# A float32 transformer trunk on one Trainium2 core: five opening blocks in each feed-forward layer instead of four, head stacks made in one step, and four other moves of work between queues

## The chip, the cores and the metric

The kernel runs on one core of a Trainium2 chip. The core has a matrix engine (PE, whose weight loads are shown as PEld), a vector engine (DVE), a scalar engine (ACT), a general engine (POOL), a queue that issues transfers (SP) and 16 DMA engines. The metric is the device time in microseconds (us) of one execution; the time before is the median of three runs. All products are in float32, made of three matmuls on rounded parts (below).

## The reference

Two layers over 512 tokens of width 1024. Each layer is a feed-forward part (SwiGLU), a token mixer, and a second feed-forward part, each between two RMS norms and with a residual:

```python
def swiglu(h, w_in, w_out):
    gu = h @ w_in
    g, u = jnp.split(gu, 2, axis=-1)
    return (jax.nn.silu(g) * u) @ w_out
...
for layer in range(DEPTH):
    g = norm_gain[layer]
    h = swiglu(rms_norm(x, g[0]), ffn_w_in[layer, 0], ffn_w_out[layer, 0])
    x = x + 0.5 * rms_norm(h, g[1])
    h = token_mixer(rms_norm(x, g[2]), mix_w_in[layer], conv_w[layer], conv_b[layer],
                    gate_bias[layer], mlstm_norm_gain[layer], mix_w_out[layer])
    x = x + rms_norm(h, g[3])
    h = swiglu(rms_norm(x, g[4]), ffn_w_in[layer, 1], ffn_w_out[layer, 1])
    x = x + 0.5 * rms_norm(h, g[5])
```

The hidden width of the feed-forward part is 2816, that is 22 tiles of 128, called f = 0 to 21 here. The mixer projects 1024 to 3600 columns, runs eight heads of windowed attention and four heads of a recurrent memory (mLSTM), and projects back.

## The kernel before

**Split numbers.** Every factor is split into a high part (ACT casts it, `hi` or `xh`) and a low part (DVE subtracts the high part from the original, `lo` or `xl`). A product is three matmuls: high by high, high by low, low by high. Weights arrive in `raw` buffers of 512 KB (three of them, and three each of `hi` and `lo`, used in turn), so a fresh load waits until an older tile is split, and a fresh split until PE is through with an older tile. The helper for the mixer's weights is `split_w` (cast L114, subtraction L115), that for the opening blocks `halves_of` (L97, L99).

**Tokens and the chain.** The 512 tokens are four tiles t = 0 to 3. At the end of each part `chain` does for each t: the norm behind the part (`post`: squares on ACT L163, gain on DVE L166, update of `xs` L170), the norm ahead of the next part (`pre`: squares on ACT L181, a power on POOL L136, scaling into `nt` on DVE L185, eight transposes `tr` on PE L191), and `put`, which copies the transposed tile out of its PSUM bank as `xh` (ACT L209), `xl` (DVE L210) and, ahead of a feed-forward part, as the exact copy `xf` (ACT L236, t 0 and 1) and as sums and differences of t and t-2 (`tq`, L228, L229). The power on POOL and two small steps before it (`rs_u`, `rs_v`) and after it (`rs_a`, `rs_y`) make the inverse root.

**The first matmul of a feed-forward part (`ffn_in`).** The first `ne` tiles f are the openings. `block(f, left)` multiplies both weight tiles of f (gate, then up) with the tokens of t 0 and 1, later `block(f, right)` with those of t 2 and 3: 48 matmuls of 256 columns each, so 96 for a tile f. The left blocks need only t 0 and 1 and can run while the chain of t 2 and 3 is made. The other tiles go through `seven`, which takes seven products of 12 matmuls, 84 in all, instead of eight, by working with sums of weights (`ws`, made on DVE in L320 to L323) and sums of tokens (`tq`, `xf`). A tile of `seven` is prepared during the one ahead of it; the first one (`now = Weights(ne)`) is prepared ahead of the loop. Its up-weight goes to a buffer `wu` in slot 17 or 19, by the parity of f:

```python
raw = chunk("wu", 17 + 2 * (f % 2)) if gu and not whole_f else raw_tile()
```

The same two slots hold `xf`: slot 17 the copy for the first half of the width, which `finish` (L228, L229, called behind the right blocks) reads last, and slot 19 the copy for the second half, whose last reader is t 3's `put` (L245).

**The mixer.** It begins with four groups of columns (`proj_nat`, PSUM name `nat`) for t 0 and 1, while t 2 and 3 of the chain are made; then `mixer_proj_T` (`projT`), which needs all tokens, then the groups for t 2 and 3 and the gates (`mixer_gates`), in which PE transposes small rows (`gnat`, L727). The attention needs for each of four head pairs a stack of keys and one of queries (`stack`, `stk`, `kst`, `qsh`, `qsl`): four transposes each, and copies out of the bank on ACT and DVE, of 64 partitions. `stack_pair` yields between keys and queries; the loop over 32 score tiles (`sc`) takes these steps at n = 2, 4, 9, 11, 16 and 18.

**Order.** A scheduler that simulates the engines lays out each engine's instructions, except in the loop over `seven`, which keeps the written order. `tc.issue_after(i)` holds what is issued in it behind instruction i.

Of the kernel before, what the change touches and what calls it, by code (L numbers as in the profile page):

```python
# [41 lines left out]
def trunk_kernel(ctx, tc, x, norm_gain, ffn_w_in, ffn_w_out, mix_w_in, conv_w, conv_b,  # L42
# [59 lines left out]
    def split_w(load, n, k4, pieces=1):  # L102
        raw = raw_tile()
        hi = wp.tile([P, 1056], F32R, tag="hi", name="hi", bufs=3)
        lo = wp.tile([P, 1056], F32R, tag="lo", name="lo", bufs=3)
        m = n * k4

        def view(w):
            return w[:, :m].rearrange("p (k c) -> p k c", k=k4)
        step = k4 // pieces  # L110
        for k in range(0, k4, step):
            r, h, l = [view(w)[:, k: k + step] for w in (raw, hi, lo)]
            load(r, k)
            A.copy(h, r)  # L114
            V.tensor_tensor(l, r, h.bitcast(F32), ALU.subtract)  # L115
        return view(hi), view(lo)
# [144 lines left out]
    def ffn_in(layer, j, xx, late=None):  # L261
# [20 lines left out]
        def block(f, c, pieces=1, after=None):  # L282
            h = h_of(f) if hts[f] is None else hts[f]
            banks = []
            for gu in range(2):
                lo_k, hi_k = halves_of(load(f, gu, pieces, True)[:, :1024], 1024, after)
                ps = psA("gu")[:, c]
                for q, w2 in enumerate((lo_k, hi_k)):
                    product(ps, w2, [x[:, 4 * q: 4 * q + 4, c] for x in (xx.h, xx.l)], q == 0)
                banks.append(ps)  # L290
# [93 lines left out]
        ne = 4  # L384
        for f in range(ne):
            block(f, left, 2 if late and f == 0 else 1, first_nt[-1] if late and f == 0 else None)
# [98 lines left out]
    def proj_nat(layer, xx, col, n, evac, tiles=range(NT), ps_of=None, per=1):  # L485
# [3 lines left out]
        for q in range(2):  # L489
            def load(dst, _, q=q):  # L490
                nc.sync.dma_start(dst, w[:, q * 4: q * 4 + 4, col: col + n])
            parts.append(split_w(load, n, 4))
# [37 lines left out]
    def mixer(layer, xx):  # L530
# [42 lines left out]
        for n, g in enumerate(groups):  # L573
            run(proj_nat(layer, xx, *g, tiles=(0, 1), per=1 + (n in (1, 2))))
# [4 lines left out]
        for n, g in enumerate(groups[1:]):  # L579
            run(proj_nat(layer, xx, *g, tiles=(2, 3), per=1 + (n < 2)))  # L580
            if n == 1:
# [39 lines left out]
        def stack_pair(hp):  # L621
# [3 lines left out]
            yield  # L625
# [4 lines left out]
            yield  # L630
# [22 lines left out]
        def opening():  # L653
            for n, _ in enumerate(heads()):
                if n == 58:
                    run(stack_pair(0))
# [179 lines left out]
    def stack(src, hp, dh, dl):  # L836
# [9 lines left out]
        else:  # L846
            for e, s, o in ((0, lo, hi), (1, hi, lo)):
# [3 lines left out]
                A.copy(dl[o, e], dl[s, e].bitcast(F32))  # L851

    def attention(stack_pair, stacks, pts, av, mask, mm):
# [54 lines left out]
        for n in range(32 + lead + 1):  # L908
            if n < 32:
                scores(n)  # L910
                if n in (2, 9, 16):
                    made = stack_pair(1 + n // 7)
                if n in (2, 4, 9, 11, 16, 18):
                    next(made)
# [24 lines left out]

    def start(t, xx=xx):  # L940
        load_x(t, 1)
        chain(t, None, xx, False)
# [4 lines left out]
    for t in range(2):  # L947
        chain(t, None, xx, False)
    late = [lambda: start(2), lambda: start(3)]
# [61 lines left out]
```

## Time and profile before

| what | value |
|---|---|
| median of three runs | 2122.14 us (2122.1 to 2124.03) |
| profiled execution | 2122.1 us, span of its instructions 2120.1 us, so 2.0 us lie around the span |
| PE busy | 2041.7 us (96%) |
| DVE busy | 1544.4 us (73%) |
| ACT busy | 1154.5 us (54%) |
| POOL busy | 253.6 us (12%) |
| DMA | 270.28 MB, mean 127 GB/s |

The page puts PE at 96%, so whatever shortens the kernel is found in the other 78 us, or in stretches in which PE is busy but slow. For that two views are read: who PE waited for, and stretches of equal length with the number of matmuls that PE did in each. The count is the better measure, since a matmul at a lowered clock is counted as busy time too. Line numbers are those of the kernel before.

### The profile page before, as it was taken

Reading aid. Unit: us, or ns where it says so; the run is one execution under the profiler, and the core shown is the slowest. Engines: PE = TensorE matmul, PEld = TensorE weight load, DVE = VectorE, ACT = ScalarE, POOL = GpSimd, SP = SyncE. Lnnn points to the kernel's source line nnn. Section 1 sums busy time; section 2 is a strip of 40 time slices with the busy share of each in tenths; the row PEclk is TensorE's granted clock in tenths of the full one; section 3 lists DMA queues with packets and bytes.
Section 4 is the critical chain, followed back from the end, with each engine's and each line's share of the span. In section 5 each row is a group of like instructions: output and inputs, shape, how many; then the busy total and the mean of one; then the engine's idle time right before and its main releaser. Section 6 shows DMA issues by size and latency. Waiting matters only on the chain. (4 is left out here: it accounts for less than half of the span.)

```text
span 2120.1 us, 35561 instructions
## 1 busy us (share of the span) xinstructions
PE 2041.7 (96%) x13870; PEld 1861.2 (88%) x13870; DVE 1544.4 (73%) x2634; ACT 1154.5 (54%) x2058; POOL 253.6 (12%) x330
## 2 busy tenths in 40 slices
PE   8899999999999989999998999999999999899998
PEld 7899988889977889998898999888899779899886
DVE  7688757685767878876687886667856677788665
ACT  5455555445665645555554555554456755455554
POOL 1000001233512100000010000003434220000000
PEclk9999999999999999999999999999999999999999
DMA  7433355541113633335663334564411235333364
GB/s 217 123 111 100 110 188 193 143 122 58 53 51 119 190 110 107 113 102 187 188 188 107 105 100 129 188 192 126 119 53 41 88 122 160 110 104 115 120 205 144
DMA packets 297566, 270.28 MB, mean 127 GB/s; under 512 B 8661, under 2 KB 267189, under 8 KB 297398
## 3 DMA queue, kind: packets, MB, share of 16 engines
q1 hardware_dynamic: 297398, 268.01, 41.8%
q8 instruction: 108, 1.77, 0.3%
q14 instruction: 60, 0.49, 0.1%
HBM read 265.88 MB, written 2.10 MB: 126 GB/s over the span
## 5 line engine op out<-in xcount | busy, mean ns | idle before, releaser
L115 DVE TENSOR_TENSOR lo<-raw,hi 128x1024 fp32r<-128x1024 f32 (+1 forms) x280 | 348.8, 1246 | 241.4 <-ACT hi L114 241.3
L114 ACT CAST hi<-raw 128x1024 fp32r<-128x1024 f32 (+1 forms) x280 | 294.5, 1053 | 311.0 <-PE o L419 225.6
L417 PE MATMUL o<-lo,hq 128*128 128x512 f32 x704 | 236.9, 394 | 0.8 <-DVE lo L115 0.8
L419 PE MATMUL o<-hi,hq 128*128 128x512 f32 x704 | 223.3, 394 | 0.0
L416 PE MATMUL o<-hi,hq 128*128 128x512 f32 x704 | 210.6, 395 | 2.5 <-ACT hq L453 2.5
L297 ACT CAST hi<-ws 128x1024 fp32r<-128x1024 f32 x144 | 151.2, 1052 | 70.9 <-ACT a L297 62.1
L255 PE MATMUL pa<-tq,hi 128*128 128x256 f32 x576 | 164.6, 286 | 22.3 <-ACT hi L297 22.3
L500 PE MATMUL nat<-hi,xh 128*128 128x256 f32 (+1 forms) x640 | 184.9, 291 | 0.0
L501 PE MATMUL nat<-lo,xh 128*128 128x256 f32 (+1 forms) x640 | 182.0, 285 | 2.9 <-DVE lo L115 2.9
L502 PE MATMUL nat<-hi,xl 128*128 128x256 f32 (+1 forms) x640 | 181.6, 285 | 0.0
L299 DVE TENSOR_TENSOR lo<-ws,hi 128x1024 fp32r<-128x1024 f32 x144 | 175.2, 1219 | 1.5 <-ACT hi L297 1.5
L257 PE MATMUL pa<-tq,lo 128*128 128x256 f32 x576 | 165.0, 286 | 1.9 <-DVE lo L299 1.9
L256 PE MATMUL pa<-tq,hi 128*128 128x256 f32 x576 | 164.8, 286 | 0.0
L255 PE MATMUL pc<-xh,hi 128*128 128x256 f32 x576 | 163.6, 284 | 0.0
L257 PE MATMUL pc<-xh,lo 128*128 128x256 f32 x576 | 163.4, 284 | 0.0
L256 PE MATMUL pc<-xl,hi 128*128 128x256 f32 x576 | 163.4, 284 | 0.0
L416 PEld LDWEIGHTS o<-hi,hq 128*128 128x128 f32 x704 | 131.9, 188 | 34.0 <-ACT hq L453 3.4
L417 PEld LDWEIGHTS o<-lo,hq 128*128 128x128 f32 x704 | 131.9, 188 | 31.5 <-DVE lo L115 1.1
L419 PEld LDWEIGHTS o<-hi,hq 128*128 128x128 f32 x704 | 132.3, 188 | 30.8
L256 PE MATMUL gu<-xl,hi 128*128 128x256 f32 x512 | 147.4, 289 | 6.6 <-DVE xl L210 6.6
L255 PE MATMUL gu<-xh,hi 128*128 128x256 f32 x512 | 146.8, 290 | 4.6 <-ACT xf L236 3.7
L257 PE MATMUL gu<-xh,lo 128*128 128x256 f32 x512 | 146.3, 288 | 0.0
(242 smaller groups left out, 5660.3 us busy)
## 6 DMA issues: line engine op xcount, KB each, us to landing
raw<-in_ffn_w_out_dram SPq DMA_DIRECT2D x176, 512.0 KB, 3.5
raw<-in_ffn_w_in_dram SPq DMA_DIRECT2D x138, 512.0 KB, 3.9
wu<-in_ffn_w_in_dram SPq DMA_DIRECT2D x68, 512.0 KB, 4.0
raw<-in_mix_w_in_dram SPq DMA_DIRECT2D x56, 512.0 KB, 3.8
raw<-in_mix_w_out_dram SPq DMA_DIRECT2D x32, 512.0 KB, 3.7
raw<-in_mix_w_in_dram SPq DMA_DIRECT2D x16, 528.0 KB, 3.7
gpost<-in_norm_gain_dram SPq DMA_DIRECT2D x6, 512.0 KB, 5.9
gpre<-in_norm_gain_dram SPq DMA_DIRECT2D x5, 512.0 KB, 4.7
```

The source lines that it names most:

```text
L114: A.copy(h, r)
L115: V.tensor_tensor(l, r, h.bitcast(F32), ALU.subtract)
L255: PE.matmul(ps, wh[:, k], xh[:, k], start=start and k == 0, stop=False, skip_group_check=True)
L256: PE.matmul(ps, wh[:, k], xl[:, k], start=False, stop=False, skip_group_check=True)
L257: PE.matmul(ps, wl[:, k], xh[:, k], start=False, stop=k == 3, skip_group_check=True)
L299: V.tensor_tensor(lo, src, fp(hi), ALU.subtract)
L416: PE.matmul(banks[t][n], a, wh[:, n], start=first, stop=False)
L417: PE.matmul(banks[t][n], a, wl[:, n], start=False, stop=False)
L419: PE.matmul(banks[t][n], b, wh[:, n], start=False, stop=end)
L500: PE.matmul(d, xh[:, k, tok], wh[:, k % 4], start=k == 0, stop=False)
L501: PE.matmul(d, xh[:, k, tok], wl[:, k % 4], start=False, stop=False)
L502: PE.matmul(d, xl[:, k, tok], wh[:, k % 4], start=False, stop=k == NK - 1)
```

## The change

- `ne` is 5 instead of 4: one more tile f in each of the four feed-forward parts goes through left and right blocks, one fewer through `seven`, and the first `Weights` is that of f = 5, whose `wu` lies in slot 19.
- At the start of the program, the chains of t 2 and 3 are held behind the last ACT instruction of t 1's chain (the second half's `xf` copy), and the low part of the first up-weight behind t 1's last DVE instruction.
- In the mixer's first four groups the low part of each second half of a weight is made on POOL instead of DVE.
- The second half of `mixer_gates` is called behind the last of the right-hand groups instead of the last but one.
- `stack_pair` makes keys and queries in one step, at n = 3, 13 and 17; in the query stacks the second copy of the low part is a subtraction on DVE (L850's form) instead of a copy on ACT (L851).

```diff
@@ -99,7 +99,7 @@
             V.tensor_tensor(lo[:, :n], src, hi[:, :n].bitcast(F32), ALU.subtract)
         return [[w[:, q: q + 512].rearrange("p (k c) -> p k c", k=4) for w in (hi, lo)] for q in range(0, n, 512)]
 
-    def split_w(load, n, k4, pieces=1):
+    def split_w(load, n, k4, sub=None, pieces=1):
         raw = raw_tile()
         hi = wp.tile([P, 1056], F32R, tag="hi", name="hi", bufs=3)
         lo = wp.tile([P, 1056], F32R, tag="lo", name="lo", bufs=3)
@@ -112,7 +112,7 @@
             r, h, l = [view(w)[:, k: k + step] for w in (raw, hi, lo)]
             load(r, k)
             A.copy(h, r)
-            V.tensor_tensor(l, r, h.bitcast(F32), ALU.subtract)
+            (sub or V).tensor_tensor(l, r, h.bitcast(F32), ALU.subtract)
         return view(hi), view(lo)
 
     def mm3(ps, lh, ll, rh, rl, start, stop):
@@ -279,11 +279,11 @@
                 hts[f] = hts[f][:, 0:512]
             return hts[f]
 
-        def block(f, c, pieces=1, after=None):
+        def block(f, c, pieces=1, after=(None, None)):
             h = h_of(f) if hts[f] is None else hts[f]
             banks = []
             for gu in range(2):
-                lo_k, hi_k = halves_of(load(f, gu, pieces, True)[:, :1024], 1024, after)
+                lo_k, hi_k = halves_of(load(f, gu, pieces, True)[:, :1024], 1024, after[gu])
                 ps = psA("gu")[:, c]
                 for q, w2 in enumerate((lo_k, hi_k)):
                     product(ps, w2, [x[:, 4 * q: 4 * q + 4, c] for x in (xx.h, xx.l)], q == 0)
@@ -381,9 +381,9 @@
             V.tensor_tensor(h[:, left], a, sil0, ALU.mult)
             V.tensor_tensor(h[:, right], u1, g1, ALU.mult)
 
-        ne = 4
+        ne = 5
         for f in range(ne):
-            block(f, left, 2 if late and f == 0 else 1, first_nt[-1] if late and f == 0 else None)
+            block(f, left, 2 if late and f == 0 else 1, (first_nt[-1], first_done[0]) if late and f == 0 else (None, None))
             if late and f < 2:
                 late[f]()
         for f in range(ne):
@@ -482,14 +482,14 @@
             V.scalar_tensor_tensor(qk[b % 4][:, b // 4, :], th[:, :512], 1.0, y[:, :512], ALU.add, ALU.mult)
         return qk
 
-    def proj_nat(layer, xx, col, n, evac, tiles=range(NT), ps_of=None, per=1):
+    def proj_nat(layer, xx, col, n, evac, tiles=range(NT), ps_of=None, sub=None, per=1):
         xh, xl = xx.h, xx.l
         w = mix_w_in[layer].rearrange("(k p) c -> p k c", p=P)
         parts = []
         for q in range(2):
             def load(dst, _, q=q):
                 nc.sync.dma_start(dst, w[:, q * 4: q * 4 + 4, col: col + n])
-            parts.append(split_w(load, n, 4))
+            parts.append(split_w(load, n, 4, sub if q else None))
         for t0 in tiles[::per]:
             ps = (ps_of or psA)("nat")
             for u in range(per):
@@ -571,14 +571,14 @@
             return go
         groups = ((3336, 264, evac_mo(1)), (2560, 256, evac_mv(0)), (2816, 256, evac_mv(1)), (3072, 264, evac_mo(0)))
         for n, g in enumerate(groups):
-            run(proj_nat(layer, xx, *g, tiles=(0, 1), per=1 + (n in (1, 2))))
+            run(proj_nat(layer, xx, *g, tiles=(0, 1), sub=G, per=1 + (n in (1, 2))))
         qk = mixer_proj_T(layer, cvt, xx)
         run(proj_nat(layer, xx, *groups[0], tiles=(2, 3)))
         gates = mixer_gates(gt)
         next(gates)
         for n, g in enumerate(groups[1:]):
             run(proj_nat(layer, xx, *g, tiles=(2, 3), per=1 + (n < 2)))
-            if n == 1:
+            if n == 2:
                 with tc.issue_after(last_ins(mybir.EngineType.PE)):
                     gates = next(gates)
 
@@ -622,12 +622,10 @@
             base = (20, 4)[hp % 2]
             ks = pair("kst", base)
             stack(kn, hp, ks, None)
-            yield
             qh = pair("qsh", base + 1)
             ql = one.tile([P, D], F32R, tag="nt", name="qsl", bufs=2).rearrange("p (a s) -> p a s", a=2)
             stack(qn, hp, qh, ql)
             stacks[hp] = (ks, qh, ql)
-            yield
 
         def projections():
             psN = banks_of(3, 4)
@@ -653,7 +651,7 @@
         def opening():
             for n, _ in enumerate(heads()):
                 if n == 58:
-                    run(stack_pair(0))
+                    stack_pair(0)
                 if n in (60, 64):
                     next(att)
                 yield
@@ -848,7 +846,7 @@
                 A.copy(dh[s, e], ps[s])
                 A.copy(dh[o, e], ps[s])
                 V.tensor_tensor(dl[s, e], ps[s], dh[s, e].bitcast(F32), ALU.subtract)
-                A.copy(dl[o, e], dl[s, e].bitcast(F32))
+                V.tensor_tensor(dl[o, e], ps[s], dh[s, e].bitcast(F32), ALU.subtract)
 
     def attention(stack_pair, stacks, pts, av, mask, mm):
         sms = {}
@@ -908,10 +906,8 @@
         for n in range(32 + lead + 1):
             if n < 32:
                 scores(n)
-                if n in (2, 9, 16):
-                    made = stack_pair(1 + n // 7)
-                if n in (2, 4, 9, 11, 16, 18):
-                    next(made)
+                if n in (3, 13, 17):
+                    stack_pair((3, 13, 17).index(n) + 1)
             m = n - lead
             if 0 <= m < 32:
                 transposes(m)
@@ -937,15 +933,19 @@
         for n in range(pieces):
             nc.sync.dma_start(xs[:, t, n * w: n * w + w], x[0, t * P: (t + 1) * P, n * w: n * w + w])
 
+    first_done = []
+
     def start(t, xx=xx):
         load_x(t, 1)
-        chain(t, None, xx, False)
+        with tc.issue_after(first_done[1]):
+            chain(t, None, xx, False)
     first_gain(gpre)
     load_x(0, 2)
     nc.sync.dma_start(idj, cst[:, 0:256])
     load_x(1, 1)
     for t in range(2):
         chain(t, None, xx, False)
+    first_done += [last_ins(mybir.EngineType.DVE), last_ins(mybir.EngineType.Activation)]
     late = [lambda: start(2), lambda: start(3)]
     for layer in range(DEPTH):
         for sub in range(3):
```

Three places in the engines' orders. The first is PE in the second feed-forward part, around the transposes of t 3 (`tr`), with the last matmuls (`gu`) of left blocks ahead of them. Before:

```order
L256 MATMUL gu<-xl,hi 128x256
L257 MATMUL gu<-xh,lo 128x256
L191 MATMUL tr<-idj,nt 128x128 x8
L255 MATMUL gu<-xh,hi 128x256 x3
L256 MATMUL gu<-xl,hi 128x256
L257 MATMUL gu<-xh,lo 128x256
```

Now:

```order
L255 MATMUL gu<-xh,hi 128x256
L256 MATMUL gu<-xl,hi 128x256
L257 MATMUL gu<-xh,lo 128x256
L191 MATMUL tr<-idj,nt 128x128 x4
L255 MATMUL gu<-xh,hi 128x256
L256 MATMUL gu<-xl,hi 128x256
L191 MATMUL tr<-idj,nt 128x128 x4
```

Before, the eight transposes stand behind all 192 matmuls of the left blocks, and the next matmuls are those of the first right block. Now they stand in two groups behind 210 and 212 matmuls of the left blocks, of which there are 240, so 28 more left-hand matmuls follow ahead of the first right block.

The second place is DVE in the same part, towards the end of the right blocks and at the first `seven` (`lo<-raw` of L99 are weights of blocks, `ht` L293 ends a block, L299 are low parts for `seven`, `xl<-xf` of L229 is `finish`, `ht` L352 belongs to the first `seven`). Before:

```order
L299 TENSOR_TENSOR lo<-raw,hi 128x1024
L229 TENSOR_TENSOR xl<-xf,xh 128x4x256
L293 TENSOR_TENSOR ht<-gu,sil 128x256
L352 TENSOR_TENSOR ht<-ha,pb 128x256
L320 TENSOR_TENSOR ws<-raw 128x512
L320 TENSOR_TENSOR ws<-wu 128x512
L321 TENSOR_TENSOR ws<-raw,wu 128x512
L299 TENSOR_TENSOR a_8190<-wu,a_8190 128x512
L322 TENSOR_TENSOR ws<-ws,raw 128x512
L323 TENSOR_TENSOR ws<-raw,ws 128x512
L299 TENSOR_TENSOR lo<-ws,hi 128x1024 x2
```

Now, beginning earlier in the right blocks:

```order
L320 TENSOR_TENSOR ws<-wu 128x512
L293 TENSOR_TENSOR ht<-gu,sil 128x256
L299 TENSOR_TENSOR a_8326<-wu,a_8326 128x512
L99 TENSOR_TENSOR lo<-raw,hi 128x1024 x2
L293 TENSOR_TENSOR ht<-gu,sil 128x256
L99 TENSOR_TENSOR lo<-raw,hi 128x1024
L321 TENSOR_TENSOR ws<-raw,wu 128x512
L322 TENSOR_TENSOR ws<-ws,raw 128x512
L99 TENSOR_TENSOR lo<-raw,hi 128x1024
L323 TENSOR_TENSOR ws<-raw,ws 128x512
L293 TENSOR_TENSOR ht<-gu,sil 128x256
L299 TENSOR_TENSOR lo<-raw,hi 128x1024
```

The sums `ws` of the first `seven` stood behind `finish` and behind the first use of that `seven` (L352); now they stand among the right blocks.

The third place is POOL at the mixer's start in the first layer (`misc` is a gain, `rs_yo` and `rs_yi` the powers of the chain for t 2 and then t 3, `smo` a gate's two steps). Before:

```order
L547 TENSOR_SCALAR misc<-misc 128x512
L136 TENSOR_TENSOR rs_yo<-rs_uo,mhalf 128x1
L560 TENSOR_TENSOR smo<-smo,misc 128x248
L136 TENSOR_TENSOR rs_yi<-rs_ui,mhalf 128x1
L561 TENSOR_TENSOR smo<-smo,misc 128x248
L560 TENSOR_TENSOR smo<-smo,misc 128x248
L561 TENSOR_TENSOR smo<-smo,misc 128x248
L136 TENSOR_TENSOR rs_yo<-rs_uo,mhalf 128x1
L136 TENSOR_TENSOR rs_yi<-rs_ui,mhalf 128x1
L560 TENSOR_TENSOR smo<-smo,misc 128x264
```

Now:

```order
L115 TENSOR_TENSOR lo<-raw,hi 128x1056
L136 TENSOR_TENSOR rs_yo<-rs_uo,mhalf 128x1
L115 TENSOR_TENSOR lo<-raw,hi 128x1024
L560 TENSOR_TENSOR smo<-smo,misc 128x248
L136 TENSOR_TENSOR rs_yi<-rs_ui,mhalf 128x1
L561 TENSOR_TENSOR smo<-smo,misc 128x248
L560 TENSOR_TENSOR smo<-smo,misc 128x248
L561 TENSOR_TENSOR smo<-smo,misc 128x248
L136 TENSOR_TENSOR rs_yo<-rs_uo,mhalf 128x1
L115 TENSOR_TENSOR lo<-raw,hi 128x1024
L136 TENSOR_TENSOR rs_yi<-rs_ui,mhalf 128x1
L115 TENSOR_TENSOR lo<-raw,hi 128x1056
```

Four subtractions of 1024 or 1056 elements per partition stand among the powers of the chain: one ahead of t 2's `rs_yo`, one behind it, and one on either side of t 3's `rs_yi`.

## The prediction

> **What bounds the kernel now.** I read the page's head, then PE's waits, then stretches of equal length, then the instructions around the two longest kinds of wait. The head:
>
> ```profile
> span 2120.1 us, 35561 instructions
> PE 2041.7 (96%) x13870; PEld 1861.2 (88%) x13870; DVE 1544.4 (73%) x2634; ACT 1154.5 (54%) x2058; POOL 253.6 (12%) x330
> ```
>
> PE is the bound, and a gain must come from PE's idle or slow time. Who it waited for (total us, times, longest):
>
> ```profile
> PE pa L255 <- ACT hi L297: 22.3, 4, 5.7
> PE tr L191 <- DVE nt L185: 12.4, 6, 4.3
> PE gu L256 <- DVE xl L210: 6.6, 2, 3.6
> PE gnat L727 <- DVE gates L721: 5.3, 4, 1.6
> PE sc L870 <- ACT qsh L849: 3.9, 4, 1.3
> PE gu L255 <- ACT xf L236: 3.7, 1, 3.7
> ```
>
> The largest comes four times, once in each feed-forward part, at the first `seven` (`pa`). Next are waits for the chain: `tr` for `nt`, `gu` for `xl`. What they cost in all, the slow time behind them included, shows in stretches of 20 us (per engine busy us and instructions, then PE's granted clock, DMA share, GB/s):
>
> ```profile
> 40.00:60.00 20.00, 20.00 (x172) 20.00 (x171) 14.30 (x19) 9.94 (x14) 0.00 (x0) 1.00 0.80 220
> 66.00:86.00 20.00, 14.10 (x99) 13.59 (x98) 13.73 (x20) 8.61 (x13) 0.00 (x0) 0.83 0.37 106
> 715.00:735.00 20.00, 16.15 (x119) 15.26 (x118) 18.71 (x31) 11.42 (x17) 1.83 (x3) 0.91 0.55 167
> 748.00:768.00 20.00, 13.83 (x97) 13.33 (x96) 13.06 (x18) 8.14 (x12) 0.00 (x0) 0.83 0.36 106
> 1082.00:1102.00 20.00, 16.06 (x121) 15.36 (x120) 18.45 (x29) 10.17 (x15) 1.83 (x2) 0.91 0.54 164
> 1114.00:1134.00 20.00, 13.88 (x101) 13.38 (x100) 13.29 (x19) 8.37 (x12) 0.00 (x0) 0.83 0.37 107
> 1765.00:1785.00 20.00, 16.26 (x109) 15.37 (x108) 17.49 (x29) 10.51 (x17) 0.02 (x1) 0.83 0.46 132
> 1798.00:1818.00 20.00, 14.02 (x94) 13.52 (x93) 12.49 (x17) 7.57 (x12) 0.00 (x0) 0.74 0.36 106
> ```
>
> The first row is full speed: 172 matmuls of 256 columns in 20 us, 0.116 us each. Each of the others lost (172 - count) x 0.116 us. The four first `seven` (99, 97, 101, 94) lost 8.5 + 8.7 + 8.3 + 9.1 = 34.5 us, more than the 22.3 of waiting, since the clock was down behind the wait. The three ends of the left blocks (119, 121, 109) lost 6.2 + 5.9 + 7.3 = 19.4.
>
> **The first `seven` and its slot.** The second part's, from SP, ACT, DVE and PE:
>
> ```profile
> 748.67 1.05 ACT L228 CAST xh<-xf 128x1024 fp32r<-128x1024 f32 x1 [1.03 <-PE gu L257]
> 751.01 6.27 SPq L272 DMA_DIRECT2D wu<-in_ffn_w_in_dram  x2
> 754.99 0.69 DVE L320 TENSOR_TENSOR ws<-wu 128x512 f32<-128x512 f32 x1 [0.95 <-DMA wu<-in_ffn_w_in_dram]
> 758.61 0.58 PE L255 MATMUL pa<-tq,hi 128*128 128x256 f32 x1 [5.71 <-ACT hi L297]
> 762.17 0.41 PE L255 MATMUL pc<-xh,hi 128*128 128x256 f32 x1
> 762.39 0.41 PE L256 MATMUL pc<-xl,hi 128*128 128x256 f32 x1
> ```
>
> The up-weight of f = 4 goes to slot 17, so its transfer is issued at 751.01, right behind the reads of `xf` by `finish`, lands 4.0 us later, and sums and cast follow. Behind the wait matmuls are 0.22 us apart, half speed. With five openings the first `seven` is f = 5, in slot 19, whose last reader is t 3's `put`. The order shows the consequence: its sums stand among the right blocks. What is late next: the cast for the second product needs the `hi` buffer of the last block's gate weight, free 24 matmuls (2.8 us) ahead of the block's end, 1 us of cast and 1.2 of subtraction, so it is there at the end. `finish` must wait for the first half of the last weight's matmuls (1.4 us ahead of the end) and takes 1.05 + 1.2, but is needed by the fourth product only, 4.2 us behind the end. So I take all 34.5 us; the floor, were the clock loss to stay, is the wait alone, 22.3.
>
> **The fifth opening's price.** f = 4 takes 96 matmuls instead of 84 in each of four parts: 48 x 0.116 = +5.6 us of PE, certain. Two more weights are fetched per part (512 KB each) and split beside it; see the rivals.
>
> **The ends of the left blocks.** Second part:
>
> ```profile
> 719.82 0.28 PE L257 MATMUL gu<-xh,lo 128*128 128x256 f32 x1
> 725.89 0.39 PE L256 MATMUL gu<-xl,hi 128*128 128x256 f32 x1 [3.01 <-DVE xl L210]
> 716.22 1.23 DVE L99 TENSOR_TENSOR lo<-raw,hi 128x1024 fp32r<-128x1024 f32 x1
> 719.42 1.41 DVE L185 SCALAR_TENSOR_TENSOR nt<-xs,rs_yi,gpre 128x512 f32<-128x512 f32 x2
> 720.74 1.22 DVE L99 TENSOR_TENSOR lo<-raw,hi 128x1024 fp32r<-128x1024 f32 x1
> 724.02 1.21 DVE L99 TENSOR_TENSOR lo<-raw,hi 128x1024 fp32r<-128x1024 f32 x1
> 725.15 1.28 DVE L210 TENSOR_TENSOR xl<-tr,xh 128x512 fp32r<-128x512 f32 x2
> ```
>
> The left blocks end at 719.9, and t 3's `xl` comes at 725.8 to 726.4, since DVE is full (18.71 of 20 us). A fifth left block gives PE 48 x 0.116 = 5.6 us of work and t 3's transposes (1 us) inside it, to 726.6. Its weights are the ninth and tenth lows (716.22, 720.74), there at 717.4 and 722.0; needed at 719.9 and 723.7. `xl` is behind the same eleven lows as before, plus one block product and one step of `tq` (by L210, 0.64 for 512 elements a partition, so some 0.3 to 0.4 and 0.6), at 727: 0.5 us is left of the wait, too short for the clock to fall (the mixer's row below). The same in the fourth part. In the third the transposes come behind all left blocks, and two more lows stand ahead of `xl`, the last of which needs a buffer that comes free as the blocks end: cast, low and first `xl` take 1.0 + 1.2 + 0.6 behind that end, less 0.9 of transposes: 2 us left, I say 2.3. Left in all 3.3, so -16.1 (bounds: -19.4, and 0 if DVE passes the whole delay on).
>
> **The start.** The first matmul waits for the first `xf` copy, and three squares of t 2 and 3, such as the first row, stand ahead of it on ACT:
>
> ```profile
> 12.96 0.63 ACT L181 ACTIVATE junk<-xs 128x512 bf16<-128x512 f32 x1
> 17.20 1.07 ACT L236 COPY xf<-tr 128x512 f32<-128x512 f32 x2
> 17.84 0.58 PE L255 MATMUL gu<-xh,hi 128*128 128x256 f32 x1 [3.69 <-ACT xf L236]
> ```
>
> They move behind: up to 3 x 0.63 = 1.9, some of which the transposes of t 1 take back; -1.5 (0 to -1.9). The late chain of t 2 then begins some 2 us later, covered by five left blocks of 5.6 us.
>
> **The mixer's start.** First layer (the second has the same), and POOL's prices:
>
> ```profile
> PE projT L120 <- DVE xl L210: 1.3, 2, 0.9
> 402.00:409.00 7.00, 4.22 (x30) 3.31 (x28) 6.37 (x7) 3.42 (x6) 4.15 (x5) 1.00 0.60 169
> 405.82 0.66 PE L191 MATMUL tr<-idj,nt 128*128 128x128 f32 x4 [1.61 <-DVE nt L185]
> 406.97 0.66 PE L191 MATMUL tr<-idj,nt 128*128 128x128 f32 x4 [0.49 <-DVE nt L185]
> L879 POOL TENSOR_SCALAR sm<-sm,dn 128x512 f32<-128x512 f32 x64 | 44.2, 693 | 126.5 <-DVE dn L878 120.5 <-DVE rs_a L128 2.2 <-DVE rs_y L130 2.0
> L477 POOL TENSOR_SCALAR y<-z,cvt 128x512 f32<-128x512 f32 x16 | 32.7, 2041 | 44.8 <-ACT z L476 39.6 <-DVE y L479 5.1
> L810 POOL TENSOR_TENSOR hs<-hs,den 128x1024 f32<-128x1024 f32 x8 | 15.2, 1898 | 2.3 <-DVE den L808 1.9
> ```
>
> PE waits 2.1 us for t 3's `nt` and 1.3 / 2 = 0.7 for its `xl`: 2.8 a layer, and the clock stays at 1.00 over waits this short. Four lows of 1.2 us leave DVE, and in the new order t 3's transposes stand 30 matmuls ahead of the groups' end. On POOL a low takes 1.9 us (L810, the nearest shape) to twice that beside a busy DVE (L477 against L879: 2.04 for 0.69). Each group gives PE 48 matmuls, 5.7 us, so a low of 4 us still comes in time but for the first and last group, and t 2's power waits behind the first. I leave 0.5 us a layer: -4.5 (-5.6 to +4, the last if each of two groups a layer waits 2 us more).
>
> **The stacks.** PE's waits for `qsh` are 3.9. For the last pair two transposes of probabilities and six matmuls of the projection now stand between the query stack and its first use, where nothing stood; some 0.5 us a layer may stay, since two more subtractions than before fall to DVE in each query stack: -3.0 (-3.9 to +2, if these hold the score chain up by a microsecond a layer).
>
> **The gates.** PE's and DVE's orders around `gnat` are the same as before, so its 5.3 us stay: 0 (within 1).
>
> **The sum**, from the profiled execution's 2122.1 us (span 2120.1, and 2.0 around it; the median is 2122.14): -34.5 + 5.6 - 16.1 - 1.5 - 4.5 - 3.0 = -54.0, so 2068.1, say 2068.
>
> **The rivals.** *DVE passes the delay on.* The fifth block puts 2 x 1.22 + 0.4 = 2.9 us on a DVE that is 18.71 and 18.45 of 20 us busy, and the waits only move: the third term is 0, 2084. For it speaks that DVE is the limit there; against it that the new lows take places in the queue that right-hand lows had. *POOL and DVE get in each other's way.* If each of the eight lows takes 4 us and holds DVE's steps of the chain up for its length, t 3's `nt` comes as late as before or later: the fifth term is +4 instead of -4.5, 2076. Against it: DVE's `nt` pair took 2.27 beside POOL where it takes 1.41 elsewhere (719.42), under a doubling:
>
> ```profile
> 404.64 2.27 DVE L185 SCALAR_TENSOR_TENSOR nt<-xs,rs_yi,gpre 128x512 f32<-128x512 f32 x2
> ```
>
> [...]
>
> *The slot is not what holds the first `seven`.* Its sums come late again for another cause: the first term is 0, 2102. Against it stand the row of 751.01 and the order. *Slower: transfers bound the blocks.* A part's ten blocks want 20 loads of 512 KB in 56.5 us, 2.8 us each. If they came one behind the other at the 4.0 that the `wu` of 751.01 took, a part would lose 20 x 1.2 = 24 us, four parts 96, and the sum is 2068 + 96 = 2164; it decides from a loss of 54.0 in 80 loads, 2.8 + 0.7 = 3.5 us a load. Against it: the DMA engines moved 220 GB/s at full PE speed (40 to 60 us), which is 2.4 us for 512 KB.
>
> **Chances.** The sum as it stands 0.6 (own range 2060 to 2077); DVE 0.18; POOL 0.1; the slot 0.05, its other cause included; transfers 0.03; something else 0.04, even on both sides. The range 2058 to 2085 takes in the first three. 0.2% of 2122 is 4.2 us, about what a measurement of this kernel can tell from no change. Faster by more: 0.95; same 0.02; slower 0.03.
>
> **What would show it.** In the profile after: no wait of `pa` for `hi` over 1 us; 165 matmuls or more in 20 us around each first `seven`; waits of `gu` for `xl` under 1 us in the second and fourth part and about 2 in the third; the first `gu` at 16.3; L115 on POOL eight times, 2 to 4 us each; no wait of projT's transposes. Wrong if 5 us waits at a first `seven` remain, or PE's waits for DVE grow elsewhere.

## The result and the profile after

The changed kernel takes 2064.84 us (median of 4 runs, 2064.62 to 2067.82) against 2122.12 of the kernel before (2121.23 to 2124.03): ratio 0.9732, 95% interval 0.9715 to 0.9749. The profiled execution took 2064.9 us, with a span of 2063.2, so 57.2 us less than the profiled execution before. In one later run, that with the lows on DVE, one of four executions took 7025.79 us; the time given there is the median of the other three.

The head of the page after, and PE's waits (total us, times, longest):

```profile
span 2063.2 us, 35640 instructions
PE 2024.2 (98%) x13918; PEld 1849.8 (90%) x13918; DVE 1541.6 (75%) x2614; ACT 1140.1 (55%) x2030; POOL 269.0 (13%) x338
```

```profile
PE tr L191 <- DVE nt L185: 6.6, 3, 4.2
PE gnat L725 <- DVE gates L719: 5.4, 4, 1.6
PE gu L255 <- ACT xf L236: 3.1, 1, 3.1
PE pt L884 <- ACT pts L889: 2.9, 4, 0.9
PE po L900 <- DVE qsl L849: 2.6, 2, 1.3
...
PE gu L256 <- DVE xl L210: 0.8, 1, 0.8
...
PE sc L868 <- ACT qsh L847: 0.5, 2, 0.2
```

There are 48 more matmuls, the fifth block's, and yet PE's busy time fell by 17.5 us: that is slow time which is no longer there (the mean granted clock of the profiled execution was 0.982 before and is 0.995 now). The longest list entry of before, `pa` waiting for `hi` (22.3 us), is gone altogether. `gu` for `xl` is 0.8 in one place where it was 6.6 in two. `gnat` is unchanged. At the stacks `sc` hardly waits for `qsh`, but two waits that were not in the list before stand there, `pt` for `pts` and `po` for `qsl`. Stretches of 20 us around the first `seven` and the ends of the left blocks (columns as before):

```profile
75.00:95.00 20.00, 20.00 (x172) 20.00 (x171) 16.82 (x25) 12.33 (x20) 0.00 (x0) 1.00 0.43 124
710.00:730.00 20.00, 20.00 (x172) 20.00 (x171) 18.42 (x26) 12.52 (x19) 1.63 (x1) 1.00 0.81 226
740.00:760.00 20.00, 20.00 (x171) 20.00 (x170) 17.48 (x26) 12.36 (x20) 0.00 (x0) 1.00 0.48 135
1064.00:1084.00 20.00, 18.61 (x156) 18.18 (x155) 16.73 (x23) 11.30 (x18) 1.42 (x1) 1.00 0.79 213
1095.00:1115.00 20.00, 20.00 (x172) 20.00 (x171) 17.01 (x25) 12.12 (x20) 0.00 (x0) 1.00 0.45 127
1730.00:1750.00 20.00, 20.00 (x172) 20.00 (x170) 17.88 (x26) 12.09 (x19) 0.00 (x0) 1.00 0.78 216
1760.00:1780.00 20.00, 20.00 (x171) 20.00 (x170) 17.04 (x25) 12.04 (x20) 0.00 (x0) 1.00 0.41 119
```

The rows of 75, 740, 1095 and 1760 hold the four first `seven`: 172, 171, 172, 171 matmuls where there were 99, 97, 101 and 94. Those of 710, 1064 and 1730 hold the ends of the left blocks: only the third part still loses anything, (172 - 156) x 0.116 = 1.9 us, and its clock no longer falls.

### The profile page after: what moved, and what is told of

The parts are those of the page before. It is cut to its first block, busy times and chain, and to the rows that moved or that the text cites. A ratio compares the mean times of both kernels' runs of the same rounds, so it can differ in the third digit from the quotient of the medians.

```text
span 2063.2 us, 35640 instructions
## 1 busy us (share of the span) xinstructions
PE 2024.2 (98%) x13918; PEld 1849.8 (90%) x13918; DVE 1541.6 (75%) x2614; ACT 1140.1 (55%) x2030; POOL 269.0 (13%) x338
## 4 chain that ended last, share of the span: by engine, by line
PE 91%; DVE 4%; ACT 2%; issue 2%; DMA 0%; SPq 0%; POOL 0%; DVEq 0%; POOLq 0%; ACTq 0%
PE o L416 9%; PE o L419 9%; PE o L417 9%; PE pa L256 6%; PE pa L257 6%; PE pa L255 6%; PE gu L256 4%; PE gu L257 4%; PE gu L255 4%; PE pc L257 3%; PE pc L256 3%; PE pc L255 3%; PE nat L500 3%; PE nat L501 3%; PE nat L502 2%; PE po L900 2%
## 5 line engine op out<-in xcount | busy, mean ns | idle before, releaser
L115 DVE TENSOR_TENSOR lo<-raw,hi 128x1024 fp32r<-128x1024 f32 (+1 forms) x272 | 338.8, 1246 | 229.5 <-ACT hi L114 228.8
L255 PE MATMUL gu<-xh,hi 128*128 128x256 f32 x640 | 180.2, 284 | 3.7 <-ACT xf L236 3.1
L256 PE MATMUL gu<-xl,hi 128*128 128x256 f32 x640 | 180.0, 283 | 0.8 <-DVE xl L210 0.8
L257 PE MATMUL gu<-xh,lo 128*128 128x256 f32 x640 | 178.8, 282 | 0.0
L299 DVE TENSOR_TENSOR lo<-ws,hi 128x1024 fp32r<-128x1024 f32 x136 | 165.9, 1220 | 3.1 <-ACT hi L297 3.1
L257 PE MATMUL pa<-tq,lo 128*128 128x256 f32 x544 | 153.1, 281 | 0.0
L257 PE MATMUL pc<-xh,lo 128*128 128x256 f32 x544 | 153.1, 281 | 0.0
L256 PE MATMUL pa<-tq,hi 128*128 128x256 f32 x544 | 153.0, 281 | 0.0
L255 PE MATMUL pc<-xh,hi 128*128 128x256 f32 x544 | 153.0, 281 | 0.0
L256 PE MATMUL pc<-xl,hi 128*128 128x256 f32 x544 | 153.0, 281 | 0.0
L255 PE MATMUL pa<-tq,hi 128*128 128x256 f32 x544 | 152.5, 280 | 0.0
```

Source lines behind the costliest of these rows:

```text
L115: (sub or V).tensor_tensor(l, r, h.bitcast(F32), ALU.subtract)
L255: PE.matmul(ps, wh[:, k], xh[:, k], start=start and k == 0, stop=False, skip_group_check=True)
L256: PE.matmul(ps, wh[:, k], xl[:, k], start=False, stop=False, skip_group_check=True)
L257: PE.matmul(ps, wl[:, k], xh[:, k], start=False, stop=k == 3, skip_group_check=True)
L299: V.tensor_tensor(lo, src, fp(hi), ALU.subtract)
```

## The experiments

Two theories on the largest term were to be told apart. *Slot*: the first `seven` waits because its up-weight shares slot 17 with `xf[0]`, so that the load is issued only behind `finish`. *Cover*: the fifth opening helps because one more block gives the loads and sums more time, in whatever slot.

### The slot alone

The kernel before, with the two slots swapped:

```
-            raw = chunk("wu", 17 + 2 * (f % 2)) if gu and not whole_f else raw_tile()
+            raw = chunk("wu", 19 - 2 * (f % 2)) if gu and not whole_f else raw_tile()
```

> The kernel before with one character sequence changed: the up-weights' slots are swapped, so that even f use slot 19 and odd f slot 17; four openings as before. Theory S (the first seven waits because its up-weight's load is held by the late read of xf[0] in slot 17): the four first seven lose nothing, no wait of pa for hi above 1 us, 2122.1 - 34.5 = 2087.6 us; the waits at the ends of the left blocks stay (19.4). Rival C (what the fifth opening gives is the longer cover of one more block, the slot is no matter): the four waits of pa stay at 5 to 6 us, about 2122 us.

Measured 2085.94 us (ratio 0.9840, 0.9823 to 0.9857), beside 2121.16 for the kernel before in the same series: -35.2 us. No wait of `pa` is left, while the ends of the left blocks stay as they were:

```profile
PE tr L191 <- DVE nt L185: 12.0, 6, 4.4
PE gu L256 <- DVE xl L210: 7.0, 2, 3.6
PE gnat L727 <- DVE gates L721: 5.4, 4, 1.6
PE sc L870 <- ACT qsh L849: 3.9, 4, 1.3
```

So the first term is there in full with no fifth block at all.

### Five openings alone

The kernel before, with `ne = 5` and nothing else:

```
-        ne = 4
+        ne = 5
```

> The kernel before with five openings and nothing else. Both theories: the waits of pa for hi go (-34.5), the fifth block costs +5.6, the ends of the left blocks give up 16 to 19 of their 19.4 us: 2122.1 - 34.5 + 5.6 - 16.1 = 2077 us, down to 2074. What is then left to the changed kernel (start, mixer start, stacks) is 9 to 12 us. If DVE passed the delay on in this kernel: 2093.

Measured 2069.60 us (0.9764, 0.9747 to 0.9780): -51.6 us, 7 more than I expected. The one digit carries nine tenths of the whole change. Where the 7 us come from is taken up below.

### The changed kernel with the late slot

The same swap in the changed kernel, which with five openings puts the first `seven`'s up-weight (f = 5) into slot 17 again:

```
-            raw = chunk("wu", 17 + 2 * (f % 2)) if gu and not whole_f else raw_tile()
+            raw = chunk("wu", 19 - 2 * (f % 2)) if gu and not whole_f else raw_tile()
```

> The changed kernel with the two slots swapped, so that with five openings the first seven's up-weight goes to slot 17 again. Theory S: the waits of pa for hi come back in all four parts, 5 to 6 us each with slow time behind them, 2064.8 + 34.5 = 2099 us. Rival C: no wait, 2065 us.

Measured 2101.14 us (0.9909, 0.9889 to 0.9930): +36.3 us against the changed kernel. The waits are back as they were:

```profile
PE pa L255 <- ACT hi L297: 22.7, 4, 5.7
```

The second part's first `seven`, its load and first sum, in the changed kernel:

```profile
720.63 0.40 SPq L272 DMA_DIRECT2D wu<-in_ffn_w_in_dram  x1
726.54 0.69 DVE L320 TENSOR_TENSOR ws<-wu 128x512 f32<-128x512 f32 x1 [1.30 <-DMA wu<-in_ffn_w_in_dram]
```

and with the swap, `finish`'s cast of `xf` ahead of them:

```profile
752.30 1.05 ACT L228 CAST xh<-xf 128x1024 fp32r<-128x1024 f32 x1 [1.03 <-PE gu L257]
754.63 6.06 SPq L272 DMA_DIRECT2D wu<-in_ffn_w_in_dram  x2
758.40 0.69 DVE L320 TENSOR_TENSOR ws<-wu 128x512 f32<-128x512 f32 x1 [0.74 <-DMA wu<-in_ffn_w_in_dram]
```

In the changed kernel the first `seven` starts at 742.3, and its first sum is made 16 us ahead of that. With the swap it starts at 753.5, and the sum is made 5 us behind that, since the load was issued only when `finish` had read `xf`. *Slot* is shown, from both sides; *cover* falls.

### Four openings with the early slot

```
-            raw = chunk("wu", 17 + 2 * (f % 2)) if gu and not whole_f else raw_tile()
+            raw = chunk("wu", 19 - 2 * (f % 2)) if gu and not whole_f else raw_tile()
...
-        ne = 5
+        ne = 4
```

> The changed kernel with four openings, the slots swapped so that the first seven's up-weight still goes to slot 19. Theory S: no waits of pa for hi; 5.6 us of matmuls saved, and the waits at the ends of the left blocks come back (19.4 less what the shorter start saves): 2064.8 - 5.6 + 19.4 = 2079 us (2073 if only half of it comes back). Rival C: the first seven's waits come back as well, 2113 us.

Measured 2080.14 us (0.9813, 0.9794 to 0.9832), +15.3. PE's waits at the ends of the left blocks come back (`tr` for `nt` 9.9, `gu` for `xl` 6.2), those of `pa` do not. So this is what the fifth block is for: it covers t 3's late chain, and its cost is less than what it covers.

### Six openings with the early slot

```
-            raw = chunk("wu", 17 + 2 * (f % 2)) if gu and not whole_f else raw_tile()
+            raw = chunk("wu", 19 - 2 * (f % 2)) if gu and not whole_f else raw_tile()
...
-        ne = 5
+        ne = 6
```

> The changed kernel with six openings, the slots swapped so that the first seven's up-weight (f = 6) goes to slot 19. If a block costs its twelve matmuls alone: 48 x 0.116 = 5.6 us more, less the 1.9 us that is left of the third part's wait with its slow time: 2064.8 + 5.6 - 1.9 = 2068.5 us. If transfers or DVE bound the blocks as their number grows: waits of gu for hi or lo appear, 2072 or more.

Measured 2069.07 us (0.9753, 0.9740 to 0.9766) beside 2064.05 for the changed kernel in the same series: +5.0. From the first `gu` to the first `o` the first, second and fourth parts grew by 1.35, 1.30 and 1.39 us, the twelve matmuls, and the third by -0.18, since its 1.9 us went. No wait of `gu` for a weight appeared: transfers do not bound twelve blocks a part either.

### The lows of the mixer's start on DVE

```
-            run(proj_nat(layer, xx, *g, tiles=(0, 1), sub=G, per=1 + (n in (1, 2))))
+            run(proj_nat(layer, xx, *g, tiles=(0, 1), per=1 + (n in (1, 2))))
```

> The changed kernel with the four second lows of each mixer start on DVE as before, none on POOL. By the prediction's term: waits of projT's transposes and of tr for nt come back, 2064.8 + 4.5 = 2069.3 us; from the two traces' stages up to the first gnat (2.3 and 2.3 us a layer against five openings alone): 2069.5. If POOL's lows bring nothing since DVE's small steps are held behind them: 2065.

Measured 2072.53 us (0.9780, 0.9758 to 0.9802): +7.7. From the first `nat` to the first `gnat` the two layers took 102.4 and 102.8 us where the changed kernel took 100.1 and 100.0, which is 5.1 and the term in question. The rest lies behind the first `o` of the output projection, which this edit does not touch: from there to the next part's first `gu` it took 80.2 and 80.0 us instead of 78.5 and 78.4, with the clock lowered in both layers (below).

### Two lows on POOL, two on DVE

In the changed kernel PE still waits 1.2 us for t 3's `nt` at each mixer's start. POOL's and DVE's rows there, first beside the second low of the first layer, then beside the fourth:

```profile
375.73 2.39 POOL L115 TENSOR_TENSOR lo<-raw,hi 128x1024 fp32r<-128x1024 f32 x1 [2.62 <-ACT hi L114]
376.06 0.17 DVE L557 TENSOR_TENSOR gt<-nat,gb 128x16 f32<-128x16 f32 x1 [0.41 <-PE nat L502]
377.29 0.85 DVE L135 SCALAR_TENSOR_TENSOR rs_ui<-pre_ss 128x1 f32<-128x1 f32 x1 [1.05 <-ACT junk L181]
```

```profile
390.12 2.45 POOL L115 TENSOR_TENSOR lo<-raw,hi 128x1056 fp32r<-128x1056 f32 x1 [0.31 <-ACT hi L114]
390.13 2.47 DVE L139 SCALAR_TENSOR_TENSOR rs_yi<-rs_ai,rs_yi 128x1 f32<-128x1 f32 x1
393.44 0.66 PE L191 MATMUL tr<-idj,nt 128*128 128x128 f32 x4 [1.22 <-DVE nt L185]
```

A step on one number a partition, elsewhere 0.15 to 0.2 us, takes 2.47, and ends when POOL's low ends; another (L135, at 377.29) takes 0.85, up to the end of POOL's low of 375.73. The sum `gt` at 376.06, one of whose operands is `nat` in PSUM, takes its 0.17 us in the middle of POOL's low. By the third low, `rs_ao` took 2.34 in the same way. So the third and fourth low were given back to DVE:

```
-            run(proj_nat(layer, xx, *g, tiles=(0, 1), sub=G, per=1 + (n in (1, 2))))
+            run(proj_nat(layer, xx, *g, tiles=(0, 1), sub=G if n < 2 else None, per=1 + (n in (1, 2))))
```

> The changed kernel with only the first two of the four second lows on POOL; the third and fourth, beside which DVE's steps on 128x1 took 2.3 to 2.5 us instead of 0.2, on DVE. Theory H (the hold by POOL is what leaves PE's wait of 1.4 us for nt in each layer): that wait goes and no DVE step of 128x1 takes over 1 us there, 2064.8 - 2.8 = 2062 us. Rival D (DVE is full there, and each low that it takes costs its 1.2 us again): half of the gain of the four lows is lost, 2064.8 + 2.3 = 2067 us.

Measured 2062.27 us (0.9735, 0.9712 to 0.9757), 2.6 below the changed kernel. The step is back at its length, though DVE now does a low of 1.25 itself just ahead of it, and PE's wait is gone (one wait of `tr` for `nt` is left, at the kernel's start):

```profile
389.50 0.22 DVE L138 SCALAR_TENSOR_TENSOR rs_ai<-rs_yi,rs_vi 128x1 f32<-128x1 f32 x1 [0.47 <-POOL rs_yi L136]
389.63 1.25 DVE L115 TENSOR_TENSOR lo<-raw,hi 128x1056 fp32r<-128x1056 f32 x1
390.80 0.15 DVE L139 SCALAR_TENSOR_TENSOR rs_yi<-rs_ai,rs_yi 128x1 f32<-128x1 f32 x1
```

```profile
PE gnat L725 <- DVE gates L719: 5.4, 4, 1.6
PE tr L191 <- DVE nt L185: 4.8, 1, 4.8
```

From the first `nat` to the first `projT` each layer takes 25.16 us where it took 26.93 and 26.88: 1.75 a layer, 3.5 in all. The hold by POOL is shown; the time of the whole kernel alone, with intervals that overlap, would not have shown it.

### The stacks as before

```
             stack(kn, hp, ks, None)
+            yield
...
-                V.tensor_tensor(dl[o, e], ps[s], dh[s, e].bitcast(F32), ALU.subtract)
+                A.copy(dl[o, e], dl[s, e].bitcast(F32))
...
-                if n in (3, 13, 17):
-                    stack_pair((3, 13, 17).index(n) + 1)
+                if n in (2, 9, 16):
+                    made = stack_pair(1 + n // 7)
+                if n in (2, 4, 9, 11, 16, 18):
+                    next(made)
```

> The changed kernel with the stacks made as before (two steps, at the old places, the second low a copy on ACT). Theory P (the prediction's term of -3.0): the waits of sc for qsh, 3.9 in all, come back: 2064.8 + 3.0 = 2068 us. Rival T (the one-step stacks only trade these waits for waits of pt for pts and of po for qsl, 5.5 us in all; what the stage of the stacks gained is the granted clock, which with five openings alone was 1.00 there as well): the stage up to the first o is 0.7 + 0.3 us a layer shorter, 2064.8 - 2.0 = 2063 us, with the granted clock at 1.00 behind the waits.

Measured 2066.45 us (0.9749, 0.9730 to 0.9769): +1.6, between the two and within what can be told. No run takes the one step and the subtraction on DVE apart. The trace shows both theories at work. Up to the first `o` it is shorter as *T* has it: from the first `stk` to the first `sc` 41.81 and 41.84 us instead of 42.12 and 42.11, from the first `po` to the first `o` 27.63 and 27.67 instead of 28.39 and 28.31, in all 1.0 a layer. From the first `o` of the output projection to the next part's first `gu` it is longer, 79.93 and 81.07 instead of 78.54 and 78.36. The waits there are the old ones:

```profile
PE sc L870 <- ACT qsh L849: 3.6, 4, 1.3
```

What is longer is the time at a lowered clock. Here are, one under the other, 20 us of the first layer's stacks, from 2 us behind the first `o` on, in the kernel before, with the slot alone, with five openings alone (these three have the old stacks in the same order), in the changed kernel, and in the one with two lows on POOL (these two have the new):

```profile
616.00:636.00 20.00, 17.15 (x80) 11.81 (x79) 10.22 (x23) 10.71 (x22) 3.44 (x5) 0.83 0.18 54
```

```profile
610.00:630.00 20.00, 17.10 (x89) 12.22 (x88) 11.24 (x26) 12.23 (x24) 3.45 (x5) 0.91 0.17 54
```

```profile
611.00:631.00 20.00, 17.10 (x102) 12.35 (x102) 12.33 (x30) 13.46 (x27) 3.77 (x6) 1.00 0.17 54
```

```profile
607.00:627.00 20.00, 17.01 (x96) 12.08 (x96) 14.70 (x33) 12.22 (x25) 3.44 (x5) 1.00 0.25 80
```

```profile
605.00:625.00 20.00, 17.00 (x85) 11.74 (x84) 13.02 (x28) 10.54 (x22) 3.44 (x5) 0.91 0.27 80
```

With the same order and the same 3.9 us of waits for `qsh`, PE did 80, 89 and 102 instructions, as the granted clock was 0.83, 0.91 and 1.00. The new form too has it both ways, 96 and 85. In this kernel it was 0.91 and 0.83 in the two layers.

These clocks are means over 20 us. In all 14 traces of this case the granted clock is either 1.00 or 0.50, and within one trace its changes lie on a grid of 3.41 us; 0.91 is one such interval at 0.50 out of 20 us, 0.83 is two. Cut at this grid, the waits of the first layer's stacks look like this, with the slot alone and then with five openings alone:

```profile
617.83:621.24 3.41, 1.44 (x6) 0.82 (x6) 1.17 (x5) 2.61 (x5) 1.36 (x2) 1.00 0.48 154
621.24:624.65 3.41, 3.12 (x11) 2.21 (x13) 1.87 (x5) 2.15 (x5) 0.69 (x1) 0.50 0.03 7
```

```profile
617.87:621.28 3.41, 1.97 (x12) 1.29 (x10) 2.05 (x5) 2.11 (x5) 1.36 (x2) 1.00 0.28 76
621.28:624.70 3.42, 2.48 (x14) 1.69 (x16) 2.03 (x5) 3.28 (x7) 0.34 (x1) 1.00 0.20 80
```

PE was busy for 1.44 us of the first interval, and the next one ran at 0.50; with 1.97 us it ran at 1.00. Over both layers of the 14 traces the clock fell behind these waits 15 times, and in the interval just ahead of the fall PE was busy for 0.37 to 0.58 of the time; the clock held 13 times, and there the least busy interval had 0.52 to 0.65. In the whole of the traces, but for the first 60 us, in which the record of the clock begins, each of the 46 intervals at 1.00 in which PE was busy for under half was followed by one at 0.50; 17 of the 62 with 0.50 to 0.66 were, and of some 8000 busier ones five, all at `gnat`.

### The projections ahead of the gates

The largest wait left in the middle of the program is `gnat`'s. The edit takes the first four steps of the projections ahead of it:

```
+        proj = projections()
+        for _ in take(proj, 4):
+            pass
+        with tc.issue_after(last_ins(mybir.EngineType.PE)):
+            gates = next(gates)
...
-        paced(opening(), 67, take(proj, 32), 32, 1)
+        paced(opening(), 67, take(proj, 28), 28, 1)
```

> The changed kernel with the first four steps of the mixer's projections (48 matmuls of 256 columns, 5.6 us) ahead of the gates' transposes (gnat) instead of behind. If gnat's waits of 5.4 us and the lower clock behind them are time lost for want of other work, they go: 2064.8 - 5.4 = 2059 us, down to 2055. If the work taken ahead is missed beside the heads later, where the scores wait: 2065 or more.

Measured 2073.28 us (0.9783, 0.9763 to 0.9802): +8.4. `gnat` no longer stands among PE's longer waits, but these do, which the changed kernel's list does not have:

```profile
PE pt L885 <- POOL sm L878: 4.3, 2, 2.1
PE st L119 <- DVE wt L786: 3.2, 2, 1.6
...
PE sc L869 <- DVE mx L874: 2.2, 2, 1.1
```

The lower clock behind `gnat` did go (the changed kernel has 6.83 us at 0.50 there in each layer, from 474.7 and from 1495.3; here no interval at 0.50 is left there), but the work is missed later beside the heads and the scores. Here the 5.4 us of waits at `gnat` were not worth the cover of a longer stretch.

### Two edits combined

Two lows on POOL, and in the first part, which has no late chain from a layer ahead, four openings with the slot still 19:

```
-            raw = chunk("wu", 17 + 2 * (f % 2)) if gu and not whole_f else raw_tile()
+            raw = chunk("wu", 17 + 2 * ((f + ne + 1) % 2)) if gu and not whole_f else raw_tile()
...
-        ne = 5
+        ne = 4 if late else 5
```

It ran beside the changed kernel once more, and beside itself with the old stacks.

> The changed kernel itself once more, beside the two that follow: 2065 us, within 2.

> The changed kernel with two edits that the runs point to: the third and fourth second low of each mixer start on DVE (-2.8 us by after_low_two), and in the first feed-forward part, which has no late chain, four openings with the first seven's up-weight still in slot 19 (12 matmuls less there, -1.4 us; in after_four_slot19 that part was 2.1 us shorter up to its first o). Sum: 2064.8 - 2.8 - 1.4 = 2060.6 us. If the first part needs the fifth block's cover: 2064 or more, with a wait of pa or gu in the first 80 us.

> The kernel combined with the stacks made as before. Theory P (the one-step stacks gain 3.0): 3 us slower than combined, 2063.6. Theory T (they cost 1.0 us a layer in the stages up to the first o, and what they seemed to gain is the clock behind a cluster of waits, which falls in some profiles of either form): 2 us faster than combined, 2058.6, where the clock is at 1.00 behind the waits in both, and up to 2 us slower where it fell here alone.

Measured: the changed kernel 2064.05 us (0.9732, 0.9719 to 0.9745); combined 2062.25 (0.9720, 0.9707 to 0.9733); combined with old stacks 2063.71 (0.9725, 0.9712 to 0.9738). The order of the first two is as expected, but the intervals overlap, so combined is not shown to be faster, and it is 1.6 over its expected sum. Against the changed kernel's first profile its trace gives 1.75 us a layer at the mixers' start again, only 0.35 in the first part (a wait of 0.9 for `lo` has come in there), and loses 1.8 and 1.9 between the first `o` and the first `gu` of the two mixers, where its clock was 0.91 and the changed kernel's 1.00. Between the two forms of the stacks the times tell nothing; up to the first `o` the old stacks are again 1.0 us a layer shorter.

## Why the prediction was right, and where it was not

The time, 2064.8, lies 3 us under the forecast of 2068 and within the likeliest case's own range. By its terms, in us:

| term | predicted | measured | from |
|---|---|---|---|
| first `seven` | -34.5 | -34.3 | stretches after: 0.2 lost; slot alone -35.2, late slot +36.3 |
| fifth block | +5.6 | +5.4 | six openings, the sixth's price: 1.35, 1.30, 1.39 a part |
| ends of the left blocks | -16.1 | -17.5 | stretches after: 1.9 lost of 19.4 |
| start | -1.5 | -0.9 | PE's wait ahead of the first `gu` |
| mixers' start | -4.5 | -5.1 | lows on DVE, first `nat` to first `gnat` |
| stacks | -3.0 | 0 to +2 | stacks as before; see below |
| clock behind the stacks' waits | - | -5.6 | five openings alone |
| sum | -54.0 | -58.0 to -56.0 | -57.2 by the profiled executions |

**The first `seven`.** The mechanism and the size were right, the slow time behind the wait included: two runs that move the load between the slots, once in each kernel, gave the same 35 to 36 us. The rival that another cause holds it up falls.

**The fifth block and the ends.** Both right within 1.4 us. The rival *DVE passes the delay on* is refuted where it was to show: the fourth part and the second lose nothing. In the third I left 2.3 us; 1.9 is there. *Transfers bound the blocks* fell too, even with six openings.

**The start.** The first `gu` came at 17.09, not at 16.3. PE's wait for `xf` differs from profile to profile: 3.7, 3.9 and 3.4 in the three kernels with the old start, and 2.4 to 3.5 in the eleven with the new one, a mean of 2.8 against 3.7. No run takes this edit back alone. Of the three squares that stood ahead of the copy on ACT (1.9 us), two stood ahead of the cast of the third weight and one behind it. In the kernel before:

```profile
15.15 1.05 ACT L97 CAST hi<-raw 128x1024 fp32r<-128x1024 f32 x1
16.57 0.64 ACT L181 ACTIVATE junk<-xs 128x512 bf16<-128x512 f32 x1
```

In the changed kernel that cast waits 0.59 us for the weight's transfer and starts only 0.13 us earlier, so the two squares ahead of it gain no more than that:

```profile
15.02 1.04 ACT L97 CAST hi<-raw 128x1024 fp32r<-128x1024 f32 x1 [0.59 <-DMA raw<-in_ffn_w_in_dram]
```

The copy starts at 16.45 instead of 17.20, and the first `gu` is earlier by as much. I had taken 1.5 of the three squares' 1.9 us, and had looked for the loss on PE alone.

**The mixers' start.** The size was near, the working was not. I had a low of up to 4 us and no hold; a low is 2.4 to 2.5, and there is a hold of 2.3 us in the chain of t 3. The rival *POOL and DVE get in each other's way* was right about the mechanism and wrong about the price: 1.75 us a layer, not 4.25. My step that failed is the reading of the `nt` pair's 2.27 us as "under a doubling", and so as evidence against a whole hold: that pair stood between several short steps of POOL and could not tell the two apart. The POOL instructions beside the pair took 0.74 to 1.19. Just ahead of the pair the trace before already had the hold, in a DVE step that takes 0.2 us elsewhere and here took 0.71, up to the end of POOL's step of 403.40:

```profile
403.40 1.00 POOL L560 TENSOR_TENSOR smo<-smo,misc 128x264 f32<-128x264 f32 x1 [1.21 <-ACT smo L559]
403.70 0.71 DVE L138 SCALAR_TENSOR_TENSOR rs_ai<-rs_yi,rs_vi 128x1 f32<-128x1 f32 x1
405.18 1.19 POOL L560 TENSOR_TENSOR smo<-smo,misc 128x264 f32<-128x264 f32 x1
```

In the trace after the hold stands alone: the step on 128x1 of 390.13, with two inputs in SBUF, took 2.47 us beside POOL's low, where it took 0.16 in the kernel before (404.44); `gt` at 376.06, with one, took its 0.17 us beside another low. No run varies the inputs alone.

**The stacks.** This is the term that failed. It priced the 3.9 us of waits for `qsh` as gone but for 1 us, 0.5 a layer for what the two more subtractions on DVE would hold up. The waits moved instead: `po` now waits 2.6 for `qsl` and `pt` 2.9 for `pts`, and 1.0 us a layer is added up to the first `o`. That is the bad end of the term's range, a microsecond a layer, and not its middle. That the sum came out all the same is luck, due to a gain that I had not seen at all: behind this cluster of waits the clock was 0.83 and 0.91 in the profile before and 1.00 in the one after, and with five openings alone, whose stacks are the old ones, it was 1.00 as well. There the stretch from the first `o` to the first `gu` fell from 82.06 and 80.72 us to 78.50 and 78.68, 5.6 in all. The clock fell with either form of the stacks, and in eleven of fourteen profiles in both layers or in neither. The changes lie on a grid of 3.41 us, and the two profiles of the changed kernel, which are of one and the same program, have that grid 0.5 and 1.8 us apart when measured from the first `o` of each layer. My estimate from this is that it matters where a cluster of waits falls against the grid, and that an edit which moves the cluster in time can gain or lose these microseconds; no run moved the cluster by itself. In the traces each of the 46 intervals at 1.00, behind the first 60 us, in which PE was busy for under half was followed by one at 0.50. What decides between 0.52 and 0.58 of PE's busy time, where both happened, stays open.

**The gates.** Unchanged, 5.3 and 5.4, as forecast.

## What to carry to other kernels

When a wait stands at the seam of two phases, ask first which buffer the late load goes to and who reads that buffer last; here one digit that changed the slot's parity was worth 35 us, and the experiment that swaps only the slots tells it from "more cover" at once. When work is moved from a busy engine to another, look at the shortest instructions of the busy one: here DVE's steps on 128x1, at 2.47 us for 0.16, showed a hold by POOL that I had not read from the `nt` pair's 2.27 for 1.41. And price the slow time behind a wait, but know that the clock behind the cluster of short waits went either way here (over 20 us 1.00 in 13 places, 0.91 or 0.83 in 15): it is no gain of the edit until more than one profile with that edit alone shows it.

## What the runs showed of the hardware that I had not expected

A DVE step on 128x1, 0.15 to 0.22 us by itself, took 2.34 and 2.47 us beside POOL subtractions of 2.52 and 2.45 us and ended with them. PE's granted clock fell to 0.50 for one or two intervals of 3.41 us (0.91 and 0.83 over 20 us) behind the waits at the stacks, of which none was longer than 1.3 us in the kernel before, and stayed at 1.00 behind the same waits with five openings alone; it cost 1.4 to 3.6 us each time it fell. None of the 46 intervals of that grid at 1.00 in which PE was busy for under half, behind the first 60 us, was followed by one at 1.00.
